# Layer 0's attention: tiles copied by GpSimd DMAs and transposed as fp32r in later turns

## The chip, the cores and the metric

The kernel runs on one core of a Trainium2 chip. The metric is the device time of one execution, in microseconds (us), as the median of several runs. The core has five engines that run their own queues in order and meet at semaphores: TensorE (PE; its weight loads are a row of their own, PEld), VectorE (DVE), ScalarE (ACT), GpSimd (POOL) and SyncE (SP, which here only issues DMAs). SBUF is the on-chip memory of 128 partitions; PSUM is where TensorE writes, in banks of 512 fp32 columns.

## The reference

Two decoder layers on 256 tokens of width 1024, in fp32. Layer 0 uses dilated attention, layer 1 a block-sparse attention (MoBA); a gated feed-forward network with a short convolution follows each. What the change touches is layer 0's attention, cut here to the core:

```python
def mixer_dilated(h, w_qkv, q_gain, k_gain, w_o, cos, sin):
    qkv = (h @ w_qkv).reshape(B, S, 3, N_DIL, N_HEADS, HEAD_DIM)   # 3 groups, 16 heads of 64
    q = apply_partial_rope(rmsnorm(qkv[:, :, 0], q_gain[:, None, :]), cos, sin)
    k = apply_partial_rope(rmsnorm(qkv[:, :, 1], k_gain[:, None, :]), cos, sin)
    v = qkv[:, :, 2]
    ...
    for g, (window, dil) in enumerate(((128, 1), (512, 4), (2048, 16))):
        o, m, d = band_attention(qb[:, g], kb[:, g], vb[:, g], dil, window)
    ...
    wgt = d * jnp.exp(m - m.max(axis=0, keepdims=True))     # the groups, merged by
    wgt = wgt / wgt.sum(axis=0, keepdims=True)              # their softmax denominators
    attn = jnp.einsum('gsh,gshd->shd', wgt, o)

def band_attention(q, k, v, dil, window):   # causal: query t sees keys t, t-dil, ..., t-window
    scores = einsum(q, k) * ATTN_SCALE, masked
    p = exp(scores - max); den = p.sum(-1); o = einsum(p, v) / den
```

Merging the three groups by their denominators is one softmax over the keys of all three, which is how the kernel computes it: 384 columns per query (256 for group 0, 64 and 64 for groups 1 and 2) with one maximum and one sum.

## The kernel before

**Precision.** A product of fp32 matrices is made of three fp32r products: each weight is split into a rounded high part (`whi`, by ACT, L109) and the rest (`wlo`, by DVE, L117), the activations likewise (`xT`). So each block of a product has three matmuls: L456, L457 and L458 (high by high, low by high, high by low).

**Turns.** The program's order is written out by hand as a series of turns. Each calls `turn(fn)`: it starts weight copies, runs what earlier turns put into the table `first` for it, finishes weight splits, runs the table `pre`, then `fn` (12 matmuls with 512 columns), then the table `post`. `at(table, dt, f, ...)` puts a call into a table dt turns ahead. Engines' queues follow this order. In `post`, a key sorts scores and probability products first, then softmax transposes, then transposes of queries and keys.

**Layer 0's attention** goes through 4 sections of 4 heads. A section has a product of queries and keys (128 tokens by 512 columns: 4 heads of queries, 4 of keys) for each of 3 groups and each of 2 chunks of tokens, 2 turns each, and products of values; in all 16 or 20 turns. What follows a product of queries and keys:

- `done`: ACT takes the squares (L539) and copies it from its PSUM bank into a `qk` tile (L533); a turn later `head_sums` (DVE, L544 to L556: sums of squares, rotation), POOL raises the sums to the power −1/2 (L318), and a turn after that `factors` scales the tile (DVE, L565).
- one turn later, in `post`, `transpose` (two in section 0): four 128x128 transposes on TensorE (L580) into one bank, f32, by a matmul with the identity; ACT copies the results out (L610) and DVE makes low parts of group 0's (L618, L616, in `second_parts`, a turn later).

The **softmax** of a section's chunk starts with `step_A` at a fixed turn (scores of group 0 at L682, of groups 1 and 2 at L691, into 4 banks), then `step_E` (DVE masks and takes the maximum, L708, ACT the exponential, L717), `step_R` (DVE divides by the sum, L724), `step_T` (12 transposes of 128x128, L732, four turns after the scores, two in section 3), `step_V` (ACT copies the transposed weights out, L739) and `step_C` (times the values, L764, at a fixed turn). Exponentials of a chunk stand in two `sm` tiles of 384 KB.

**PSUM**: tiles named `acc` rotate over three banks, those named `S` over four, `O` has one. A product of queries and keys and a set of four transposes each take the next `acc` bank (in section 0 some take `S`). A new tile has to wait until the last reader of the tile three before it is done.

The rest of the code around the change, with the profile's line numbers:

Of the kernel before, what the change touches and what calls it, by code (L numbers as in the profile page):

```python
# [10 lines left out]
F32 = mybir.dt.float32  # L11
F32R = mybir.dt.float32r
# [5 lines left out]
P = 128  # L18
D = 1024
# [39 lines left out]
def r32(ap):  # L59
    return ap.bitcast(F32)  # L60
# [81 lines left out]
def trunk_kernel(ctx, tc, x, a_w_qkv, a_w_o, b_w_qkv, b_w_o, ffn_norm, ffn_w_up, ffn_w_down, pack, mask_a, mask_b,  # L142
# [72 lines left out]
    def at(table, dt, fn, *args):  # L215
        table.setdefault(now[0] + dt, []).append((fn, args))
# [35 lines left out]
        nc.scalar.activation(sp.tile([P, 1], F32, name="wt", bufs=1), ones, func)  # L252

    def gain_row(l):
        g = cp.tile([P, D], F32, name="gain", bufs=1)
        nc.gpsimd.dma_start(g, ffn_norm[l:l + 1, :].to_broadcast([P, D]))
        return g

# [20 lines left out]
    load_T(RAW + 1, 1)  # L279


    pk = cp.tile([P, PK], F32, name="pk")
    nc.sync.dma_start(pk[:, 0:264], pack[:, 0:264])
    mA = cp.tile([P, 768], F32, name="mA")
    mB = cp.tile([P, 384], F32, name="mB")
# [3 lines left out]
    cwT = [pk[:, 264 + l * 176:440 + l * 176] for l in range(2)]  # L289
# [160 lines left out]
    def new_acc():  # L450
        return ps.tile([P, 512], F32, name="acc", bufs=3)
# [9 lines left out]
    def attention(xT, norms, ng, g0, mask):  # L461
# [63 lines left out]
        def qk_block(sec, g, res, rq):  # L525
# [33 lines left out]
            def factors(c, qk, rs):  # L559

                h0 = 0 if dil else HS
                if not dil:
                    rq[c] = rs
                t3 = qk.rearrange("p (h d) -> p h d", d=HD)[:, h0:]
                nc.vector.tensor_mul(t3, t3, rs[:, h0:, None].to_broadcast([P, 8 - h0, HD]))  # L565
                at(post, 2 if dil and sec == 0 else 1, transpose, c, qk)

            def transpose(c, qk):
                if c == 0:
                    if dil and g > 0:  # L570
                        res[g] = [bp.tile([P, 2, 2, P], F32R, name="t0", bufs=TB) for _ in range(2)]
                    elif dil:
                        res[g] = [bp.tile([P, 2, 2, S], F32R, name="kT", bufs=QB) for _ in range(2)]
                    else:
                        res[g] = (bp.tile([P, 2, 2, P], F32R, name="t0", bufs=TB),
                                  bp.tile([P, 2, 2, P], F32R, name="t0", bufs=TB),
                                  bp.tile([P, 2, 2, S], F32R, name="kT", bufs=QB))
                tp = ps.tile([P, 512], F32, name="S", bufs=4) if dil and sec == 0 and g < 2 else new_acc()
                for i in range(4):
                    nc.tensor.transpose(tp[:, i * P:(i + 1) * P], qk[:, i * P:(i + 1) * P], ident)  # L580
                q = tp[:, 0:2 * P].rearrange("p (r t) -> p r t", r=2)
                k = tp[:, 2 * P:4 * P].rearrange("p (r t) -> p r t", r=2)
                gk = gqk[:, g0 + g:g0 + g + 1]
                cs = slice(c * P, (c + 1) * P)

                copies, subs = [], []

                def plain(t0):
                    copies.extend(((r32(t0[:, 0]), q, 1.0), (r32(t0[:, 1]), k, gk)))

                def split(hi, lo, src, scale):
                    copies.append((hi, src, 1.0 if scale is None else scale))
                    subs.append((hi, lo, src, scale))


                if dil and g > 0:
                    plain(res[g][c])
                elif dil:
                    qT, kT = res[g]
                    split(kT[:, :, 0, cs], kT[:, :, 1, cs], k, gk)  # L600
                    split(qT[:, 0, :, cs], qT[:, 1, :, cs], q, None)
                else:
                    t0, q1, kT = res[g]
                    split(kT[:, :, 0, cs], kT[:, :, 1, cs], k, gk)
                    if c == 0:
                        plain(t0)
                    else:
                        split(q1[:, 0], q1[:, 1], q, None)
                for o, src, scale in copies:
                    nc.scalar.activation(o, src, AF.Copy, scale=scale)  # L610
                at(first, 1, second_parts, subs)
# [46 lines left out]

            yield from product(done)

        O, weights, starts = {}, {}, []

        def step_A(sec, c, heads, qkT, v, rq):

# [33 lines left out]
            at(first, 2, step_R, heads, sm, den, n)  # L698
            at(post, (2 if sec == NSEC - 1 else 4) if wide else 3 if not dil and sec == NSEC - 1 else 2, step_T, sec, c, heads, v, sm, n)

        def step_E(c, heads, rq, place, n, part, sm, den, mx, nb_):

            t = bp.tile([P, 768], F32, name="sm", bufs=2)
            these = range(len(heads))[part]
            sm.extend(t[:, i * n:(i + 1) * n] for i in range(len(these)))
            for i in these:
                s2, o = place[i]
                nc.vector.tensor_tensor_reduce(  # L708
                    out=sm[i], in0=s2[:, o:o + n], in1=mask[:, c * moff:c * moff + n],
                    op0=ALU.add, op1=ALU.max, scale=1.0, scalar=-3.0e38, accum_out=mx[:, i:i + 1])  # L710
# [6 lines left out]
                nc.scalar.activation(sm[i], sm[i], AF.Exp, bias=nb_[:, i:i + 1],  # L717
                                     scale=1.0 if dil else rq[c][:, heads[i]:heads[i] + 1], accum_out=den[:, i:i + 1])

        def step_R(heads, sm, den, n):  # L720
            rd = sp.tile([P, 4], F32, name="rd", bufs=2)
            nc.vector.reciprocal(rd[:, 0:len(heads)], den[:, 0:len(heads)])
            for i in range(len(heads)):
                nc.vector.tensor_scalar(sm[i], sm[i], rd[:, i:i + 1], None, op0=ALU.mult)  # L724

        def step_T(sec, c, heads, v, sm, n):
            tot = n * len(heads)
            Tp = [ps.tile([P, 512], F32, name="S", bufs=4) for _ in range((tot + 511) // 512)]
            for b in range(tot // P):
                o = b % 4 * P  # L730
                i = b * P % n
                nc.tensor.transpose(Tp[b // 4][:, o:o + P], sm[b * P // n][:, i:i + P], ident)  # L732
            at(pre, 1, step_V, sec, c, heads, v, Tp, tot)

        def step_V(sec, c, heads, v, Tp, tot):
# [286 lines left out]
    at(post, 12, nc.sync.dma_start, pk[:, 264:PK], pack[:, 264:PK])  # L1022
    at(post, 20, nc.sync.dma_start, mB, mask_b)
    aT = attention(xT, norms, NG, 0, mA)
    for c in range(2):
        nc.gpsimd.dma_start(xr[:, c, :], x[0, c * P:(c + 1) * P, :])
    xT = new_T()
# [108 lines left out]
```

## Time and profile before

| | |
|---|---|
| median of 3 runs | 762.57 us (762.27 to 762.66) |
| span of the profiled execution (its own time is not listed beside it) | 760.9 us |
| PE busy | 756.4 us, 99% |
| PEld busy | 635.4 us, 84% |
| DVE busy | 582.3 us, 77% |
| ACT busy | 506.0 us, 67% |
| POOL busy | 69.8 us, 9% |
| transposes of queries and keys (L580) | 128, 272 to 275 ns each |
| transposes of softmax weights (L732) | 144, 275 ns each |

Busy time of PE counts matmuls from start to modelled end; they overlap, so a matmul's duration is longer than the time from its start to the next one's. In a row of a timeline stand the start, the busy time, engine, line, operation, what is written and read (`out<-moving,stationary` for a matmul), the shape, the count, and in brackets how long the engine had been idle before and what released it. The rows of the groups end with busy time, mean duration in ns, and idle time ahead of them.

### The profile page before, as it was taken

How to read it: one execution, taken by the hardware profiler on the slowest of the kernel's cores; microseconds unless marked ns; L12 is line 12 of the kernel's file. 1: busy time of each engine (PE TensorE's matmuls, PEld its weight loads, DVE VectorE, ACT ScalarE, POOL GpSimd, SP SyncE). 2: the span in 40 equal slices, each digit the busy share in tenths (PEclk: the TensorE clock that was granted, in tenths of full speed). 3: DMA queues.
4: the chain of work that ended last, by engine and by line, in shares of the span. 5: the costliest groups of instructions: out<-in, count | busy, mean ns of one | idle time of the engine just before them, and what ended most of it. 6: DMA issues, size and time to landing. Idle time of an engine off the chain costs nothing.

```text
span 760.9 us, 12046 instructions
## 1 busy us (share of the span) xinstructions
PE 756.4 (99%) x4394; PEld 635.4 (84%) x4394; DVE 582.3 (77%) x1123; ACT 506.0 (67%) x887; POOL 69.8 (9%) x77
## 2 busy tenths in 40 slices
PE   9999999999999999999999999999999999999998
PEld 8888888888888888888888888787778888888886
DVE  6887875975786566997887787978866798877874
ACT  7778666757776457676666656777765677566660
POOL 0330120320131000000000001112000000000000
PEclk9999999999999999999999999999999999999999
DMA  9947462562746436487666553743646368666621
GB/s 293 332 141 251 132 186 80 181 217 65 231 158 223 132 90 194 146 251 215 192 193 183 195 190 116 231 139 112 190 116 185 119 186 247 200 178 200 191 100 56
DMA packets 149452, 133.83 MB, mean 176 GB/s; under 512 B 5904, under 2 KB 134544, under 8 KB 149392
## 3 DMA queue, kind: packets, MB, share of 16 engines
q1 hardware_dynamic: 148816, 130.96, 56.0%
q0 software_dynamic: 576, 2.10, 0.7%
q8 instruction: 34, 0.56, 0.3%
q14 instruction: 26, 0.21, 0.1%
HBM read 131.99 MB, written 1.05 MB: 175 GB/s over the span
## 4 chain that ended last, share of the span: by engine, by line
PE 99%; DVE 0%; issue 0%
PE acc L887 14%; PE acc L456 13%; PE acc L458 13%; PE acc L457 13%; PE acc L890 8%; PE S L940 5%; PE S L941 5%; PE S L942 5%; PE O L887 5%; PE O L890 3%; PE O L764 2%; PE acc L513 2%; PE S L732 2%; PE acc L580 2%; PE S L682 2%; PE O L513 1%
## 5 line engine op out<-in xcount | busy, mean ns | idle before, releaser
L117 DVE TENSOR_TENSOR wlo<-raw,whi 128x1024 fp32r<-128x1024 f32 x236 | 283.5, 1217 | 7.0 <-ACT whi L109 6.6
L109 ACT ACTIVATE whi<-raw 128x1024 fp32r<-128x1024 f32 x236 | 244.3, 1054 | 5.7 <-DMA raw<-in_a_w_qkv_dram 2.3
L456 PE MATMUL acc<-whi,xT 128*128 128x512 f32 x424 | 171.8, 405 | 0.0
L458 PE MATMUL acc<-wlo,xT 128*128 128x512 f32 x424 | 165.8, 391 | 0.0
L457 PE MATMUL acc<-whi,xT 128*128 128x512 f32 x424 | 165.4, 390 | 0.0
L887 PE MATMUL acc<-xT,whi 128*128 128x512 f32 x480 | 119.3, 390 | 0.0
L887 PEld LDWEIGHTS acc<-xT,whi 128*128 128x128 f32 x480 | 88.3, 188 | 17.2
L458 PEld LDWEIGHTS acc<-wlo,xT 128*128 128x128 f32 x424 | 79.6, 188 | 17.5
L456 PEld LDWEIGHTS acc<-whi,xT 128*128 128x128 f32 x424 | 79.7, 188 | 16.8 <-issue 1.2
L457 PEld LDWEIGHTS acc<-whi,xT 128*128 128x128 f32 x424 | 79.9, 188 | 14.7
L318 POOL TENSOR_TENSOR rs_y<-rs_v,mhalf 128x8 f32<-128x8 f32 x32 | 53.7, 1681 | 210.9 <-DVE rs_v L316 208.0
L890 PEld LDWEIGHTS acc<-xT,wlo 128*128 128x128 f32 x480 | 65.5, 190 | 4.7
L940 PE MATMUL S<-whi,kT 128*128 128x512 f32 x174 | 68.2, 392 | 0.0
L941 PE MATMUL S<-whi,kT 128*128 128x512 f32 x174 | 68.1, 391 | 0.0
L942 PE MATMUL S<-wlo,kT 128*128 128x512 f32 x174 | 67.7, 389 | 0.0
L890 PE MATMUL acc<-xT,wlo 128*128 128x256 f32 x480 | 66.9, 282 | 0.0
L911 DVE SCALAR_TENSOR_TENSOR qk<-sm,pk,qk 128x255 f32<-128x255 f32 (+1 forms) x160 | 66.6, 476 | 0.4 <-ACT qk L908 0.3
L900 DVE TENSOR_TENSOR sm<-acc,pT 128x256 f32<-128x256 f32 x60 | 25.4, 423 | 46.9 <-ACT pT L899 46.9
L908 ACT ACTIVATE qk<-sm,pk 128x256 f32<-128x256 f32 x80 | 47.8, 598 | 4.0 <-DVE sm L900 3.7
L924 ACT ACTIVATE kT<-qk 128x512 fp32r<-128x512 f32 x22 | 13.9, 633 | 41.2 <-DVE qk L919 41.2
L887 PE MATMUL O<-xT,whi 128*128 128x512 f32 x160 | 40.2, 393 | 0.0
L942 PEld LDWEIGHTS S<-wlo,kT 128*128 128x128 f32 x174 | 32.7, 188 | 7.0
(167 smaller groups left out, 927.5 us busy)
## 6 DMA issues: line engine op xcount, KB each, us to landing
raw<-in_ffn_w_up_dram SPq DMA_DIRECT2D x80, 512.0 KB, 4.2
raw<-in_a_w_qkv_dram SPq DMA_DIRECT2D x144, 256.0 KB, 4.3
raw<-in_ffn_w_down_dram SPq DMA_DIRECT2D x44, 512.0 KB, 3.8
raw<-in_b_w_qkv_dram SPq DMA_DIRECT2D x48, 256.0 KB, 3.5
raw<-in_a_w_o_dram SPq DMA_DIRECT2D x8, 512.0 KB, 3.8
raw<-in_ffn_w_up_dram SPq DMA_DIRECT2D x16, 256.0 KB, 3.6
raw<-in_b_w_o_dram SPq DMA_DIRECT2D x8, 512.0 KB, 3.8
xr<-in_x_dram POOLq DMA_DIRECT2D x2, 512.0 KB, 5.9
```

The source lines that it names most:

```text
L109: self.nc.scalar.activation(hi, raw, AF.Copy)
L117: self.nc.vector.tensor_sub(lo, self.raw[self.done], r32(hi))
L318: nc.gpsimd.tensor_tensor(y, v, mhalf[:, 0:n], op=ALU.pow)
L456: nc.tensor.matmul(acc, T[:, k, 0, cs], hi, start=first, stop=False)
L457: nc.tensor.matmul(acc, T[:, k, 1, cs], hi, start=False, stop=False)
L458: nc.tensor.matmul(acc, T[:, k, 0, cs], lo, start=False, stop=last)
L887: nc.tensor.matmul(acc, hi[:, k], xT[:, k].rearrange("p j t -> p (j t)"), start=(k == 0), stop=False)
L890: nc.tensor.matmul(acc[:, S:2 * S], lo[:, k], xT[:, k, 0], start=False, stop=(k == 7))
L911: nc.vector.scalar_tensor_tensor(o[:, d:S], u[:, 0:S - d], cw[:, first_tap + b:first_tap + b + 1], o[:, d:S], op0=ALU.mult, op1=ALU.add)
L940: nc.tensor.matmul(o, acts[f][:, 0, cs], hi[:, sl], start=start, stop=False)
L941: nc.tensor.matmul(o, acts[f][:, 1, cs], hi[:, sl], start=False, stop=False)
L942: nc.tensor.matmul(o, acts[f][:, 0, cs], lo[:, sl], start=False, stop=stop)
```

## The change

In sections 1 to 3 the scaled tile of queries and keys is no longer transposed where it stands. `move` copies it by a DMA that POOL issues (256 KB, SBUF to SBUF) into another `qk` tile of type fp32r, and the transposes read that, two turns later (three for group 0), with an identity of type fp32r. So they stand four turns (five for group 0) behind `done`'s product rather than three. Group 2 of section 3 and all of section 0 stay as they were. In sections 0 to 2 `step_M` copies the two divided softmax tiles in the same way (384 KB each, into new tiles `pL`), and `step_T` comes 5 turns (first chunk) or 6 (second) after the scores rather than 4. Section 3's softmax and layer 1 stay.

Beside this, tiles are put together to make room: the identity is drafted in a `qk` buffer and cast to fp32r by DVE, the gain row takes a `kT` buffer, the small tables a `pT` buffer, both masks one buffer, and layer 1's tables of rotations are made at turn 12, not 40.

```diff
-    ident = cp.tile([P, P], F32, name="ident")
-    make_identity(nc, ident)
+    draft = bp.tile([P, 512], F32, name="qk", bufs=5)[:, 0:P]
+    make_identity(nc, draft)
+    ident_r = cp.tile([P, P], F32R, name="ident")
+    nc.vector.tensor_copy(ident_r, draft)
+    ident = r32(ident_r)
...
-                at(post, 2 if dil and sec == 0 else 1, transpose, c, qk)
-
-            def transpose(c, qk):
+                if not dil or sec == 0 or g == 2 and sec == NSEC - 1:
+                    at(post, 2 if dil and sec == 0 else 1, transpose, c, qk, ident)
+                else:
+                    at(post, 0, move, c, qk)
+
+            def move(c, qk):
+                moved = bp.tile([P, 512], F32R, name="qk", bufs=5)
+                nc.gpsimd.dma_start(r32(moved), qk)
+                at(post, 2 if g else 3, transpose, c, moved, ident_r)
+
+            def transpose(c, qk, one):
...
+                to = tp if one is ident else tp.bitcast(F32R)
                 for i in range(4):
-                    nc.tensor.transpose(tp[:, i * P:(i + 1) * P], qk[:, i * P:(i + 1) * P], ident)
+                    nc.tensor.transpose(to[:, i * P:(i + 1) * P], qk[:, i * P:(i + 1) * P], one)
...
-            at(post, (2 if sec == NSEC - 1 else 4) if wide else 3 if not dil and sec == NSEC - 1 else 2, step_T, sec, c, heads, v, sm, n)
+            moved = [] if dil and sec < NSEC - 1 else None
+            at(first, 2, step_R, heads, sm, den, n, moved)
+            at(post, (2 if sec == NSEC - 1 else 5 + c) if wide else 3 if not dil and sec == NSEC - 1 else 2, step_T, sec, c, heads, v, sm, n, moved)
...
+        def step_M(sm, n, moved):
+            for i in range(0, len(sm), 2):
+                t = bp.tile([P, 768], F32R, name="pL", bufs=2)
+                moved.extend(t[:, j * n:(j + 1) * n] for j in range(2))
+                nc.gpsimd.dma_start(r32(t), box_of[id(sm[i + 1])])
...
-                nc.tensor.transpose(Tp[b // 4][:, o:o + P], sm[b * P // n][:, i:i + P], ident)
+                to = Tp[b // 4][:, o:o + P]
+                nc.tensor.transpose(to if moved is None else to.bitcast(F32R), src[b * P // n][:, i:i + P], one)
...
-    at(post, 40, gain_tables, 1, nc.gpsimd)
+    at(post, 12, gain_tables, 1, nc.gpsimd)
```

Where instructions move, the order of each engine's queue tells. First TensorE in section 1, at the end of the product of group 2's first chunk (`acc_1179` before, `acc_1191` after) and the start of its second chunk's (`acc_1262`, `acc_1264`); numbers tell tiles of one name apart. Before:

```order
L456 MATMUL acc_1179<-whi_1051,xT_126 128x512
L457 MATMUL acc_1179<-whi_1051,xT_126 128x512
L458 MATMUL acc_1179<-wlo_1052,xT_126 128x512
L456 MATMUL acc_1262<-whi_948,xT_126 128x512
L457 MATMUL acc_1262<-whi_948,xT_126 128x512
L458 MATMUL acc_1262<-wlo_949,xT_126 128x512
```

After:

```order
L459 MATMUL acc_1191<-whi_1055,xT_128 128x512
L460 MATMUL acc_1191<-whi_1055,xT_128 128x512
L461 MATMUL acc_1191<-wlo_1056,xT_128 128x512
L592 MATMUL acc_1239<-ident_90,qk_1166 128x128 x4
L459 MATMUL acc_1264<-whi_959,xT_128 128x512
L460 MATMUL acc_1264<-whi_959,xT_128 128x512
```

Four transposes of group 1 now stand between the two products; the `acc` tiles taken around here are 1111, 1124 (transposes), 1179, 1209 (transposes), 1262 before, and 1191, 1204 (transposes), 1239 (transposes), 1264 after. So the tile three before the second chunk's is a set of transposes before, and the first chunk's product after.

Next VectorE in section 2, at the scaling of group 1's second chunk (`qk_1817` before, `qk_1841` after). Before:

```order
L565 TENSOR_TENSOR qk_1750<-qk_1750,rs_y_1767 128x512
L618 SCALAR_TENSOR_TENSOR kT_1702<-acc_1789,gqk_125,kT_1702 128x2x128
L616 TENSOR_TENSOR kT_1701<-acc_1789,kT_1701 128x2x128
...
L117 TENSOR_TENSOR wlo_1797<-raw_1538,whi_1796 128x1024
L117 TENSOR_TENSOR wlo_1800<-raw_1570,whi_1799 128x1024
L565 TENSOR_TENSOR qk_1817<-qk_1817,rs_y_1831 128x512
L117 TENSOR_TENSOR wlo_1822<-raw_1646,whi_1821 128x1024
```

After:

```order
L117 TENSOR_TENSOR wlo_1821<-raw_1569,whi_1820 128x1024
L117 TENSOR_TENSOR wlo_1824<-raw_1601,whi_1823 128x1024
L568 TENSOR_TENSOR qk_1841<-qk_1841,rs_y_1857 128x512
L630 SCALAR_TENSOR_TENSOR kT_1808<-acc_1883,gqk_127,kT_1808 128x2x128
L628 TENSOR_TENSOR kT_1807<-acc_1883,kT_1807 128x2x128
L117 TENSOR_TENSOR wlo_1848<-raw_1673,whi_1847 128x1024
```

The low parts of group 0's second chunk (`acc_1789`, `acc_1883`) have moved from behind one scaling to behind the next, and in section 2 their bank is the one that group 2's second product takes over.

Last ScalarE at the end of section 1, where group 2's transposes are copied out (`t_1342`, `t_1391`: second chunk; `v`: values copied out, `xT<-O`: the attention's output of section 0). Before:

```order
L633 ACTIVATE v_1370<-acc,rn_r_392 128x256
L636 ACTIVATE v_797<-acc,rn_r_392 64x256 x2
L610 ACTIVATE t_1342<-acc 128x256
L610 ACTIVATE t_1342<-acc,gqk 128x256
L109 ACTIVATE whi<-raw 128x1024 x2
L444 ACTIVATE xT<-O 128x2x2x64 x2
L717 ACTIVATE sm,den<-sm,nbias 128x384 x4
```

After:

```order
L109 ACTIVATE whi<-raw 128x1024 x2
L447 ACTIVATE xT<-O 128x2x2x64 x2
L731 ACTIVATE sm,den<-sm,nbias 128x384 x4
L645 ACTIVATE v_1520<-acc,rn_r_394 128x256
L648 ACTIVATE v_859<-acc,rn_r_394 64x256 x2
L622 ACTIVATE t_1391<-acc 128x256
L622 ACTIVATE t_1391<-acc,gqk 128x256
```

The second chunk's copies have moved from ahead of two weight copies, the output and the exponentials to behind them.

More of the change, by code (lines that the diff above doesn't have):

```diff
@@ L254, in gain_row @@
     def gain_row(l):
-        g = cp.tile([P, D], F32, name="gain", bufs=1)
+        g = bp.tile([P, D], F32, name="kT", bufs=QB)
         nc.gpsimd.dma_start(g, ffn_norm[l:l + 1, :].to_broadcast([P, D]))
@@ L279, in trunk_kernel @@
     load_T(RAW + 1, 1)
-    pk = cp.tile([P, PK], F32, name="pk")
+    pk = bp.tile([P, 768], F32, name="pT", bufs=4)
     nc.sync.dma_start(pk[:, 0:264], pack[:, 0:264])
-    mA = cp.tile([P, 768], F32, name="mA")
-    mB = cp.tile([P, 384], F32, name="mB")
+    taps = cp.tile([P, PK - 264], F32, name="taps")
+    mA = bp.tile([P, 768], F32, name="mask", bufs=1)
     gcol = pk[:, 0:8].rearrange("p (j g) -> p j g", j=2)
@@ L288, in trunk_kernel @@
     gbf = pk[:, 136:264].rearrange("p (m d) -> p m d", d=16)
-    cwT = [pk[:, 264 + l * 176:440 + l * 176] for l in range(2)]
+    cwT = [taps[:, l * 176:176 + l * 176] for l in range(2)]
     CG = cp.tile([P, 2, 4, 2, 16], F32, name="CG")
@@ L659, in v_last @@
             yield from product(done)
-        O, weights, starts = {}, {}, []
+        O, weights, starts, box_of = {}, {}, [], {}
         def step_A(sec, c, heads, qkT, v, rq):
@@ L697, in step_A @@
                 at(pre if i and sec < NSEC - 1 else first, 1, step_E, c, heads, rq, place, n, slice(i, i + 2 if wide else len(heads)), sm, den, mx, nb_)
-            at(first, 2, step_R, heads, sm, den, n)
-            at(post, (2 if sec == NSEC - 1 else 4) if wide else 3 if not dil and sec == NSEC - 1 else 2, step_T, sec, c, heads, v, sm, n)
+            moved = [] if dil and sec < NSEC - 1 else None
+            at(first, 2, step_R, heads, sm, den, n, moved)
+            at(post, (2 if sec == NSEC - 1 else 5 + c) if wide else 3 if not dil and sec == NSEC - 1 else 2, step_T, sec, c, heads, v, sm, n, moved)
         def step_E(c, heads, rq, place, n, part, sm, den, mx, nb_):
@@ L705, in step_E @@
             sm.extend(t[:, i * n:(i + 1) * n] for i in range(len(these)))
+            box_of[id(sm[-1])] = t
             for i in these:
@@ L718, in step_E, with step_R @@
                                      scale=1.0 if dil else rq[c][:, heads[i]:heads[i] + 1], accum_out=den[:, i:i + 1])
-        def step_R(heads, sm, den, n):
+        def step_R(heads, sm, den, n, moved):
             rd = sp.tile([P, 4], F32, name="rd", bufs=2)
@@ L724, in step_R, with step_T @@
                 nc.vector.tensor_scalar(sm[i], sm[i], rd[:, i:i + 1], None, op0=ALU.mult)
-        def step_T(sec, c, heads, v, sm, n):
+            if moved is not None:
+                at(post, 0, step_M, sm, n, moved)
+        def step_M(sm, n, moved):
[3 more added lines that the diff above has]
+                nc.gpsimd.dma_start(r32(t), box_of[id(sm[i + 1])])
+        def step_T(sec, c, heads, v, sm, n, moved):
+            src, one = (sm, ident) if moved is None else (moved, ident_r)
             tot = n * len(heads)
@@ L1018, in trunk_kernel @@
     at(post, 6, norm.sums)
-    at(post, 40, gain_tables, 1, nc.gpsimd)
+    at(post, 12, gain_tables, 1, nc.gpsimd)
     at(post, 7, norm.factors)
     at(post, 8, nc.sync.dma_start, mA, mask_a)
-    at(post, 12, nc.sync.dma_start, pk[:, 264:PK], pack[:, 264:PK])
-    at(post, 20, nc.sync.dma_start, mB, mask_b)
+    at(post, 12, nc.sync.dma_start, taps, pack[:, 264:PK])
     aT = attention(xT, norms, NG, 0, mA)
+    mB = bp.tile([P, 768], F32, name="mask", bufs=1)
+    at(post, 20, nc.sync.dma_start, mB[:, 0:384], mask_b)
     for c in range(2):
```

## The prediction

> **What bounds the kernel now.** I read the busy line and the chain of waits first, then the groups by form on TensorE (PE), then the timelines around the places that the change touches.
>
> ```profile
> span 760.9 us, 12046 instructions
> PE 756.4 (99%) x4394; PEld 635.4 (84%) x4394; DVE 582.3 (77%) x1123; ACT 506.0 (67%) x887; POOL 69.8 (9%) x77
> PE 99%; DVE 0%; issue 0%
> 135.00:140.00 5.00, 5.00 (x62) 4.03 (x61) 4.97 (x11) 3.15 (x6) 3.65 (x5) 1.00 0.73 233
> ```
>
> PE is busy for 756.4 of 760.9 us and the chain is 99% PE: whatever shortens PE's own work shortens the kernel, one for one, and any microsecond in which PE has to wait is lost one for one. The last line (a five-microsecond window in layer 0: length, then PE, PEld, DVE, ACT, POOL busy, granted clock, DMA share, GB/s) shows that DVE, at 77% on average, is full here (4.97 of 5.00). So in layer 0 a wait for DVE is near even where none shows. The clock is 1.00 there, so durations are at full speed.
>
> **The gain: cheaper transposes.** The moved sections have 16 blocks of queries and keys with 4 transposes each, and 6 softmax steps with 12 each: 136 transposes become fp32r. A transpose multiplies the tile (stationary) by a moving identity of 128 columns, so its price is that of 128 moving columns, unless loading the stationary operand takes longer.
>
> ```profile
> L764 PE MATMUL O<-pT,v 128*64 128x128 f32 x224 | 17.2, 277 | 0.0
> L764 PE MATMUL O<-pT,v 128*64 128x64 f32 x128 | 6.4, 221 | 0.0
> L887 PE MATMUL acc<-xT,whi 128*128 128x512 f32 x480 | 119.3, 390 | 0.0
> L890 PE MATMUL acc<-xT,wlo 128*128 128x256 f32 x480 | 66.9, 282 | 0.0
> 67.62 0.39 PE L458 MATMUL acc<-wlo,xT 128*128 128x512 f32 x1
> 67.85 1.47 PE L732 MATMUL S<-ident,sm 128*128 128x128 f32 x12
> 69.39 0.40 PE L457 MATMUL acc<-whi,xT 128*128 128x512 f32 x1
> 97.88 0.39 PE L458 MATMUL acc<-wlo,xT 128*128 128x512 f32 x1
> 98.11 0.39 PE L456 MATMUL acc<-whi,xT 128*128 128x512 f32 x1
> 287.28 1.12 PE L890 MATMUL acc<-xT,wlo 128*128 128x256 f32 x8
> 288.24 0.60 PE L867 MATMUL S<-ident,qk 128*128 128x128 f32 x4
> ```
>
> A duration is not the price, since matmuls overlap; the price is the pitch from start to start. Two fp32r products with 512 columns stand 0.23 us apart (97.88 to 98.11). From 67.62 to 69.39, 12 f32 transposes lie among two such products (one at 67.62, one just ahead of 69.39): 1.77 − 2 × 0.23 = 1.31 us, 109 ns each. Eight fp32r products with 256 columns take 288.24 − 287.28 = 0.96 us, 120 ns each. A column costs (277 − 221)/64 = 0.875 ns in f32 and (390 − 282)/256 = 0.42 ns in fp32r. So an fp32r transpose with 128 columns should have a pitch of 120 − 128 × 0.42 = 66 ns, going down from the row with 256 columns, or 109 − 128 × (0.875 − 0.42) = 51 ns, going down from the f32 transposes. I take 66, since its row is of the new type: 136 × 43 = **−5.9 us**; with 51 it is −7.9.
>
> ```profile
> L732 PEld LDWEIGHTS S<-ident,sm x144: 138/140/143, 67.6 to 558.2; 128*128 128x128 f32 x144
> L890 PEld LDWEIGHTS acc<-xT,wlo x480: 187/192/192, 287.1 to 740.6; 128*128 128x128 f32 x160
> 112.77 2.90 PE L764 MATMUL O<-pT,v 128*64 128x128 f32 x64
> ```
>
> What can undo this is the load. The f32 transposes' loads take 140 ns each and the fp32r ones 192 ns (minimum, median, maximum in each row), and yet those with 192 run at a pitch of 120. So loads overlap, and the pitch that they allow lies at or below 120, not in view. The nearest rows below are the 64 small products of L764: 2.90/64 = 45 ns each with a 64-column load, so 90 ns for 128 columns at most. The gain then has a floor: pitch 120 would cost 136 × 11 = +1.5 us, pitch 90 would bring −2.6. [...]
>
> **The new waits on PSUM banks.** Moving a transpose also changes which earlier tile its neighbours inherit a bank from. There are three "acc" banks, in rotation. In sections 1 and 3 the last product of group 2 (second chunk) took over the bank of an early transpose; now two transposes stand between, and it takes over the bank of the product that ended just ahead of it. PE must wait until ACT has copied that product out (squares, then copy).
>
> ```profile
> 98.64 0.64 ACT L539 ACTIVATE sq<-acc 128x512 f32<-128x512 f32 x1
> 99.11 0.65 ACT L533 ACTIVATE qk<-acc 128x512 f32<-128x512 f32 x1
> 219.66 0.39 PE L458 MATMUL acc<-wlo,xT 128*128 128x512 f32 x1
> 220.89 0.65 ACT L533 ACTIVATE qk<-acc 128x512 f32<-128x512 f32 x1
> ```
>
> The product's last matmul ends at 97.88 + 0.39 = 98.27, the copy at 99.76: 1.49 us, and in section 3 the same (220.05, 221.54). The four transposes that PE has in between fill 4 × 66 ns = 0.26, and the first matmul needs some 0.1 to start: 1.35 us lost, in two sections **+2.7 us**. Bounds: 1.2 each, or 2.4 each if ACT is one weight copy late (L109, below). Queued behind the waiting matmul is all of PE.
>
> In section 2 the same product waits for DVE instead: for the two subtractions L618, L616 on the moved transposes of group 0, which now stand behind one more scaling (L565).
>
> ```profile
> 135.50 0.97 PE L682 MATMUL S<-kT 64*128 64x256 f32 x12
> 139.65 0.55 DVE L708 CUSTOM_DVE_ANT_0 sm<-S,mA 128x384 f32<-128x384 f32 x1
> 145.27 0.18 DVE L722 RECIPROCAL rd<-den 128x4 f32<-128x4 f32 x1 [1.38 <-ACT sm L717]
> 149.65 0.69 DVE L565 TENSOR_TENSOR qk<-qk,rs_y 128x512 f32<-128x512 f32 x1
> 154.78 0.68 DVE L565 TENSOR_TENSOR qk<-qk,rs_y 128x512 f32<-128x512 f32 x1
> 153.70 0.39 PE L456 MATMUL acc<-whi,xT 128*128 128x512 f32 x1
> 117.88 0.38 ACT L610 ACTIVATE t<-acc 128x256 f32<-128x256 f32 x1 [6.40 <-PE acc L580]
> ```
>
> Count from the scores at 135.50, section 1's second chunk. PE came to the product in question at 153.70, 18.2 us later; of the 24 f32 transposes in between, 12 move out and 12 get cheaper: 18.2 − 24 × 0.109 + 12 × 0.066 = 16.4. DVE has the same instructions as before from the first mask (139.65) to the end of the scaling (154.78 + 0.68 = 155.46): 15.8 us. It began 4.15 us after the scores, because it was behind; ACT's stall of 6.40 us ahead of it (117.88, ACT in its queue ahead of the weight copies that DVE needs) goes, since those transposes now stand behind the scores and their copies behind the exponentials. So I let DVE begin 1.3 us after the first score matmul (0.97 us of scores and a start): 1.3 + 15.8 + 0.25 (PE's restart) = 17.4, against 16.4: **+1.0 us**. Bounds: 0 (the 1.38 us that DVE waited at 145.27 shrink) and 3.8 (DVE begins as late as before).
>
> **The copies.** Each moved tile goes through a DMA of 256 KB (16 of them, queries and keys) or 384 KB (12, softmax), issued by POOL, which is 91% idle. What one takes is not in the trace; the nearest rows:
>
> ```profile
> xr<-in_x_dram POOLq DMA_DIRECT2D x2, 512.0 KB, 5.9
> gain<-in_ffn_norm_dram POOLq DMA_DIRECT2D x2, 512.0 KB, 7.2
> L109 ACT ACTIVATE whi<-raw 128x1024 fp32r<-128x1024 f32 x236 | 244.3, 1054 | 5.7 <-DMA raw<-in_a_w_qkv_dram 2.3
> out_dram<-xr SPq DMA_DIRECT2D x3, 256.0 KB, 2.0
> 80.18 0.97 PE L682 MATMUL S<-kT 64*128 64x256 f32 x12
> 92.61 0.69 DVE L565 TENSOR_TENSOR qk<-qk,rs_y 128x512 f32<-128x512 f32 x1
> 127.02 1.41 DVE L724 TENSOR_SCALAR sm<-sm,rd 128x384 f32<-128x384 f32 x4
> 128.61 1.47 PE L732 MATMUL S<-ident,sm 128*128 128x128 f32 x12
> ```
>
> 256 KB landed in 2.0 us from SP's queue, 512 KB in 5.9 to 7.2 from POOL's; I take 4.0, midway to the lower. The tightest place is section 1: the scaling ends at 92.61 + 0.69 = 93.30, less 0.81 for a pair L618, L616 that now stands behind it: 92.5. PE ends the product ahead at 98.27 − 24 × 0.109 + 8 × 0.066 = 96.2 (counted from the scores at 80.18, as above) and then waits for its bank until 97.5 anyway. So a landing of up to 97.5 − 0.26 − 92.5 = 4.7 us costs nothing more, and each microsecond beyond costs one, in sections 1 and 3. In section 2 the same transposes have 1 us more. The softmax copies start at 127.02 + 1.41 = 128.4; PE took the tiles at 128.61 and now takes them a turn (12 products, 2.73 us) or two later: 131.3 for the first chunk, where 4.0 us lets them land at 132.4, but the 6.40 us that ACT no longer stalls lie in this very chain. Nothing, at most 1.1 in each of sections 1 and 3; the second chunk has 2.7 more. ACT's copies of later products into the five "qk" buffers, and DVE's next masks into "sm", wait for landings of three products and ten turns ago: nothing.
>
> **What else moves.**
>
> ```profile
> 3.52 0.48 DVE L397 SCALAR_TENSOR_TENSOR xT<-xr,xT 128x256 fp32r<-128x256 f32 x1 [2.52 <-ACT xT L396]
> L318 POOL TENSOR_TENSOR rs_y<-rs_v,mhalf 128x8 f32<-128x8 f32 x32 | 53.7, 1681 | 210.9 <-DVE rs_v L316 208.0 <-DVE rb L554 2.9
> q1 hardware_dynamic: 148816, 130.96, 56.0%
> ```
>
> The draft of the identity and its cast stand at the start, where DVE waits 2.52 us for data; the gain row, the small tables and masks in shared buffers load when these are idle; gain_tables(1) fills POOL at turn 12 rather than 40, where POOL waits for DVE (208.0 us ahead of L318 alone): nothing in each case. The 28 copies add 16 × 256 + 12 × 384 KB = 8.7 MB to the 131 MB of the weights' queue, whose packets fill 56% of the DMA engines' time.
>
> **Sum** against the profiled execution, of which the page gives the span alone: −5.9 + 2.7 + 1.0 = −2.2 us, 760.9 → 758.7. The median of the runs, 762.57, lies 1.7 above that span; I take these 1.7 us to stay: **760.4 us**. Its own range is 758.5 to 763 (pitch 51 and no wait in section 2; both waits at their ends and a late softmax copy). A change within 0.2%, 1.5 us, cannot be told from none.
>
> **Rivals.**
>
> *Loads set the pitch* (slower). If a transposed fp32r load cannot be started every 66 ns, the waits stay and the gain doesn't. For it: 192 against 140 ns in the load rows; and 128 f32 columns cost 128 × 0.875 = 112 ns, so that at 109 a limit just below could not be seen. Against it: 45 ns for a 64-column load. At an unchanged 109 the sum is 0 + 3.7: 766.3; at 120 it is 767.8. It decides from a pitch of 109 − 3700/136 = 82 ns on: beyond that the kernel is slower than before.
>
> *Copies land late* (slower). Landing at 7.2, the gain row: 2.5 us more in sections 1 and 3, 1.5 in section 2: 766.9; at 5.9 it is 763.0. I take 764.9; it decides from 5.8 us on. [...] Against: half the bytes. [...]
>
> *The waits don't come* (faster still). DVE and ACT run ahead, so that the bank is free 1.2 us after each product and section 2 doesn't wait, at a pitch of 51: −7.9 + 2.4 = −5.5, 757.1.
>
> **Chances.** Forecast .48, loads .20, late copies .15, no waits .12, anything else .05 (half of it slower). Faster by over 0.2% (below 761.0): .33 of the forecast, .12, .01: .46. Within: .13 of the forecast, .04 of the copies, .03 of the loads, .02: .22. Slower (above 764.1): .17 of the loads, .11 of the copies, .02 of the forecast, .02: .32. From 757.4 to 767.4 the range takes in the rivals but for their ends, and leaves out about 2 in 10.
>
> **What the profile after would show.** [...] PE idle ahead of the first matmul of group 2's second chunk, 1.3 us for ACT's copy in sections 1 and 3, about 1 for DVE in section 2; if it is the transposes that wait for a DMA, copies were late. ACT without its 6.40 us stall. The DMA rows of "qk" and "pL" near 4 us to landing. I would be wrong above all if the pitch is over 82 ns or the landing over 5.8 us.

## The result and the profile after

The changed kernel takes 767.91 us as the median of 6 runs, against 762.5 before; the ratio is 1.006 (95% interval 1.0049 to 1.0071). In a second job it took 768.25 (766.99 to 769.54) beside 762.69, ratio 1.0074 (1.0061 to 1.0087). The forecast was 760.4, with 767.4 as the upper end of the range. The first profile fell on an execution whose granted clock was 0.85 from end to end (span 826.3), so the lines below are from the changed kernel in the second job. Its line numbers are those of the changed code: L592 and L756 are the transposes (L580 and L732 before), L459 to L461 the products (L456 to L458).

The head of the page and the chain of waits:

```profile
span 766.5 us, 12167 instructions
PE 755.8 (99%) x4394; PEld 632.7 (83%) x4394; DVE 583.3 (76%) x1124; ACT 508.0 (66%) x887; POOL 83.5 (11%) x105
PE 88%; DMA 5%; DVE 3%; issue 2%; ACT 2%; POOL 0%; SPq 0%; DVEq 0%; POOLq 0%; ACTq 0%
```

The span is 5.6 us longer while PE's busy time is no longer than before (756.4 then). The chain was 99% PE; now 12% of it runs through others. Busy shares alone would not show this: the chain does. PE's waits (us in all, times, longest):

```profile
PE acc L592 <- DMA qk<-qk: 3.5, 2, 2.4
PE acc L592 <- DVE kT L628: 2.1, 1, 2.1
```

Before, layer 0's sections had none. PE's timeline has them at the three places that the prediction named, at the end of the product of group 2's first chunk in sections 1, 2 and 3, but ahead of the transposes of group 1's first chunk that stand there:

```profile
96.31 0.39 PE L461 MATMUL acc<-wlo,xT 128*128 128x512 f32 x1
98.81 0.51 PE L592 MATMUL acc<-ident,qk 128*128 128x128 f32 x4 [2.12 <-DVE kT L628]
...
99.92 0.55 PE L459 MATMUL acc<-whi,xT 128*128 128x512 f32 x1
100.27 0.63 PE L460 MATMUL acc<-whi,xT 128*128 128x512 f32 x1
...
103.57 0.64 PE L756 MATMUL S<-ident,pL 128*128 128x128 f32 x6
...
154.71 0.39 PE L461 MATMUL acc<-wlo,xT 128*128 128x512 f32 x1
156.14 0.51 PE L592 MATMUL acc<-ident,qk 128*128 128x128 f32 x4 [1.04 <-DMA qk<-qk]
...
221.32 0.39 PE L461 MATMUL acc<-wlo,xT 128*128 128x512 f32 x1
224.13 0.51 PE L592 MATMUL acc<-ident,qk 128*128 128x128 f32 x4 [2.42 <-DMA qk<-qk]
```

In section 1 the profile names DVE's subtraction L628, but it was the copy there too. These are L628 in sections 1 and 2:

```profile
98.35 0.42 DVE L628 TENSOR_TENSOR kT<-acc,kT 128x256 fp32r<-128x256 f32 x1
155.79 0.41 DVE L628 TENSOR_TENSOR kT<-acc,kT 128x256 fp32r<-128x256 f32 x1
```

In section 1 it ended at 98.77, and the copy, issued at 93.57, landed after 5.1 us, at 98.7: the two nearly coincide. In section 2 the transposes started at 156.14, before L628 had ended (156.20), so they do not need it there; and in section 1 PE starts 0.04 us behind its end, where elsewhere it takes 0.14 to start behind such a subtraction (152.77 to 152.91 and 98.72 to 98.86 in kernels below). In the f32 version below, the profile names the copy in all three places.

From start to start, less the usual 0.23 us, PE loses 2.27, 1.20 and 2.58 us: 6.05. Then something that was in no part of the prediction's sum: from 99.92 to 103.57 nine products take 3.65 us, 0.41 each rather than 0.23. The stretches' row says why (length, busy times, then the granted clock):

```profile
100.10:103.40 3.30, 3.30 (x9) 2.52 (x9) 3.12 (x8) 1.07 (x2) 1.66 (x1) 0.50 0.95 304
103.60:107.00 3.40, 3.40 (x24) 2.97 (x23) 0.00 (x0) 2.48 (x5) 0.57 (x1) 1.00 0.77 252
```

From 1.2 us after the first wait on, PE's clock stood at 0.50 for about 3.4 us, and 3.65 − 9 × 0.23 = 1.6 us were lost. The gain is there too, at less than half its size. Twelve fp32r softmax transposes between two products, and four of queries and keys:

```profile
70.90 0.39 PE L461 MATMUL acc<-wlo,xT 128*128 128x512 f32 x1
71.13 1.14 PE L756 MATMUL S<-ident,pL 128*128 128x128 f32 x12
72.11 0.47 PE L459 MATMUL acc<-whi,xT 128*128 128x512 f32 x1
72.41 0.40 PE L460 MATMUL acc<-whi,xT 128*128 128x512 f32 x1
...
230.88 0.39 PE L461 MATMUL acc<-wlo,xT 128*128 128x512 f32 x1
231.11 0.46 PE L592 MATMUL acc<-ident,qk 128*128 128x128 f32 x4
231.41 0.46 PE L459 MATMUL acc<-whi,xT 128*128 128x512 f32 x1
231.71 0.39 PE L460 MATMUL acc<-whi,xT 128*128 128x512 f32 x1
```

72.41 − 70.90 − 2 × 0.23 = 1.05 us, 88 ns each; 231.71 − 230.88 − 2 × 0.23 = 0.37, 93 ns each, where f32 had 109 and 111. That is 72 × 21 + 64 × 18 ns = 2.7 us. The account of this execution: −2.7 + 6.05 + 1.6 = +4.95; another 0.6 was lost in the first 26 us of the program, ahead of the sections; measured +5.6.

### The profile page after: what moved, and what is told of

Same layout as the page of the kernel before. It is cut to its first block, busy times and chain, and to the rows that moved or that the text cites. A ratio compares the mean times of both kernels' runs of the same rounds, so it can differ in the third digit from the quotient of the medians.

```text
span 826.3 us, 12167 instructions
## 1 busy us (share of the span) xinstructions
PE 820.5 (99%) x4394; PEld 653.3 (79%) x4394; DVE 584.9 (71%) x1124; ACT 511.6 (62%) x887; POOL 83.6 (10%) x105
## 3 DMA queue, kind: packets, MB, share of 16 engines
HBM read 131.99 MB, written 1.05 MB: 161 GB/s over the span
## 4 chain that ended last, share of the span: by engine, by line
PE 99%; ACT 0%; DVE 0%; issue 0%
PE acc L911 15%; PE acc L459 14%; PE acc L461 13%; PE acc L460 13%; PE acc L914 7%; PE S L965 5%; PE S L964 5%; PE S L966 5%; PE O L911 5%; PE O L914 2%; PE O L788 2%; PE acc L516 2%; PE S L756 2%; PE S L694 1%; PE acc L592 1%; PE S L460 1%
## 5 line engine op out<-in xcount | busy, mean ns | idle before, releaser
L459 PE MATMUL acc<-whi,xT 128*128 128x512 f32 x424 | 182.7, 431 | 0.2
L461 PE MATMUL acc<-wlo,xT 128*128 128x512 f32 x424 | 176.7, 417 | 0.0
L460 PE MATMUL acc<-whi,xT 128*128 128x512 f32 x424 | 176.4, 416 | 0.0
L911 PE MATMUL acc<-xT,whi 128*128 128x512 f32 x480 | 130.4, 417 | 0.0
L461 PEld LDWEIGHTS acc<-wlo,xT 128*128 128x128 f32 x424 | 81.4, 192 | 24.0
L459 PEld LDWEIGHTS acc<-whi,xT 128*128 128x128 f32 x424 | 81.4, 192 | 23.7 <-issue 1.4
L460 PEld LDWEIGHTS acc<-whi,xT 128*128 128x128 f32 x424 | 81.8, 193 | 20.7
L965 PE MATMUL S<-whi,kT 128*128 128x512 f32 x174 | 72.8, 419 | 0.0
L964 PE MATMUL S<-whi,kT 128*128 128x512 f32 x174 | 72.5, 417 | 0.0
L966 PE MATMUL S<-wlo,kT 128*128 128x512 f32 x174 | 72.2, 415 | 0.0
L935 DVE SCALAR_TENSOR_TENSOR qk<-sm,taps,qk 128x255 f32<-128x255 f32 (+1 forms) x160 | 66.6, 477 | 0.4
L932 ACT ACTIVATE qk<-sm,taps 128x256 f32<-128x256 f32 x80 | 47.8, 597 | 2.9 <-DVE sm L924 2.7
L923 ACT ACTIVATE pT<-acc 128x256 f32<-128x256 f32 x60 | 22.8, 380 | 34.8 <-PE acc L914 33.1
L547 DVE TENSOR_REDUCE qssq<-sq 128x8 f32<-128x512 f32 x32 | 21.8, 682 | 31.8 <-ACT sq L542 31.8
```

Source lines behind the costliest of these rows:

```text
L459: nc.tensor.matmul(acc, T[:, k, 0, cs], hi, start=first, stop=False)
L460: nc.tensor.matmul(acc, T[:, k, 1, cs], hi, start=False, stop=False)
L461: nc.tensor.matmul(acc, T[:, k, 0, cs], lo, start=False, stop=last)
L911: nc.tensor.matmul(acc, hi[:, k], xT[:, k].rearrange("p j t -> p (j t)"), start=(k == 0), stop=False)
L935: nc.vector.scalar_tensor_tensor(o[:, d:S], u[:, 0:S - d], cw[:, first_tap + b:first_tap + b + 1], o[:, d:S], op0=ALU.mult, op1=ALU.add)
L964: nc.tensor.matmul(o, acts[f][:, 0, cs], hi[:, sl], start=start, stop=False)
```

## The experiments

Each is the changed kernel with the edit shown, unless another base is named.

**The changed kernel again.**

> The changed kernel itself, once more, for a profile at full clock (the first one was taken at a granted clock of 0.85, span 826.3). Theory W (new waits eat the gain): fp32r transposes stand 60 to 75 ns apart, and PE waits some 8 us in layer 0, for copies and for banks. Rival L (loads set the pitch): the transposes stand 100 ns or more apart and the waits come to 3 to 4 us. Rival K (clock): the waits come to under 4 us and the transposes are cheap, but the granted clock falls below 1.00 in stretches and costs the rest. Time 765.4 to 769 in all.

768.25. None of the three theories had it whole: the pitch lies between W's and L's, the waits between W's 8 us and L's 4, and K's fall of the clock comes on top. The five runs' granted clocks were 0.995 to 0.998, and the times followed them: 766.99 at 0.998, 769.54 at 0.996. Two runs of the first job at 1.000 took 765.45 and 765.92. That is about 762.5 − 2.7 + 6.05 = 765.9, the account without a half-clock stretch. So the scatter of this kernel, 4 us where the kernel before has under 1, follows the granted clock (0.995 to 1.000): as I read it, half-clock stretches that come or stay away. The profile of one execution, at 0.997, has one.

**Copies kept, fp32r left out.**

```diff
-                moved = bp.tile([P, 512], F32R, name="qk", bufs=5)
-                nc.gpsimd.dma_start(r32(moved), qk)
-                at(post, 2 if g else 3, transpose, c, moved, ident_r)
+                moved = bp.tile([P, 512], F32, name="qk", bufs=5)
+                nc.gpsimd.dma_start(moved, qk)
+                at(post, 2 if g else 3, transpose, c, moved, ident)
...
-                t = bp.tile([P, 768], F32R, name="pL", bufs=2)
+                t = bp.tile([P, 768], F32, name="pL", bufs=2)
...
-            src, one = (sm, ident) if moved is None else (moved, ident_r)
+            src, one = (sm, ident) if moved is None else (moved, ident)
...
-                nc.tensor.transpose(to if moved is None else to.bitcast(F32R), src[b * P // n][:, i:i + P], one)
+                nc.tensor.transpose(to, src[b * P // n][:, i:i + P], one)
```

> All copies and all moved turns stay, but the copied tiles are f32 and are transposed as f32. W: the waits stay and the gain of 136 x 43 ns goes, some 772 (a little less, since later PE waits less). L: no different from the changed kernel, 767. K: if the clock falls because of the fp32r transposes, full clock and 764 to 768.

768.85 (768.48 to 771.48), clock 0.995 to 1.000. The half-clock stretches are here too (0.51 from 99.9 to 103.4 us; 0.92 over 100 to 120 us and 0.91 over 220 to 240), so fp32r doesn't cause them. PE waits for the copy in all three places:

```profile
PE acc L592 <- DMA qk<-qk: 4.9, 3, 2.1
```

The medians are only 0.6 us apart, but they lie at different granted clocks (0.997 for the changed kernel, 0.999 here). At a granted clock of 1.000 two runs of this kernel took 768.48 and 768.55, and two of the changed one 765.45 and 765.92, in another job: so fp32r is worth some 2.8 us in this order too, as far as two runs each can tell.

**fp32r kept, copies and turns left out.** DVE's own scaling and division write the fp32r tiles (`to` is a new `qk` tile, `o` part of a `pL` tile), and `transpose` and `step_T` run in the turns of before.

```diff
-                nc.vector.tensor_mul(t3, t3, rs[:, h0:, None].to_broadcast([P, 8 - h0, HD]))
+                nc.vector.tensor_mul(to, t3, rs[:, h0:, None].to_broadcast([P, 8 - h0, HD]))
...
-                    at(post, 0, move, c, qk)
+                    at(post, 1, transpose, c, moved, ident_r)
...
-                nc.vector.tensor_scalar(sm[i], sm[i], rd[:, i:i + 1], None, op0=ALU.mult)
+                nc.vector.tensor_scalar(o, sm[i], rd[:, i:i + 1], None, op0=ALU.mult)
```

> No copies and the turns of before: DVE's scaling (queries and keys) and division (softmax) write an fp32r tile themselves, which rounds the values, and the same 136 transposes are fp32r. W: the gain without the waits, 762.5 - 5.9 = 756.6 (755 to 758). L: 762 to 764. K: 757 to 761, with the granted clock below 1.00 in the runs that are late.

760.52 (760.05 to 760.72), ratio 0.997 (0.996 to 0.9981): a gain of 2.2, not 5.9. From the start of 12 of its transposes to the next product it is 0.98 us (67.45 to 68.43), as in the changed kernel (71.13 to 72.11), so the copies have no part in that. Waits of 0.2 us each at two places make up most of the rest to 2.7.

**The same tiles, in the change's turns.** Base: the kernel just above.

```diff
-                    at(post, 1, transpose, c, moved, ident_r)
+                    at(post, 2 if g else 3, transpose, c, moved, ident_r)
...
-            at(post, (2 if sec == NSEC - 1 else 4) if wide else 3 if not dil and sec == NSEC - 1 else 2, step_T, sec, c, heads, v, sm, n, moved)
+            at(post, (2 if sec == NSEC - 1 else 5 + c) if wide else 3 if not dil and sec == NSEC - 1 else 2, step_T, sec, c, heads, v, sm, n, moved)
```

> No copies (DVE writes the fp32r tiles), but all transposes in the turns of the change. Theory B (the turns alone: banks and DVE) has the prediction's waits: about 1.1 to 1.4 us each in sections 1 and 3 for ACT's copy of the product ahead, 0 to 1 in section 2, none for a DMA; 762.7 - 2.75 (the gain that the traces show) + 2.5 to 3.5 = 762.5 to 763.5. Theory D (the copies' landing is all of the waits): no wait, 760.0, like the kernel with the turns of before.

763.05 (ratio 1.0005, 0.9996 to 1.0014). The turns alone give back the whole gain, as theory B had it; PE's waits:

```profile
PE acc L459 <- ACT qk L536: 1.8, 2, 0.9
PE acc L459 <- DVE kT L626: 1.0, 1, 1.0
```

These are the prediction's bank waits, in their three places: 0.9 us each where it had 1.35, and 1.0 where it had 1.0. So 2.8 us are the banks'; what the copies add to that, up to the changed kernel's 6.05, the next experiments show.

**Softmax alone; queries and keys alone.** The first:

```diff
-                if not dil or sec == 0 or g == 2 and sec == NSEC - 1:
+                if True:
```

> Only the softmax tiles are copied (12 copies of 384 KB) and transposed as fp32r a turn or two later; queries and keys as before. W, with the loss in the queries' and keys' part as the prediction had it: 762.5 - 72 x 0.043 = 759.4, no wait. If the loss lies in the softmax part (late copies, S banks held longer): 763 or more. L: 762.5 to 764.

The second:

```diff
-            moved = [] if dil and sec < NSEC - 1 else None
+            moved = None
...
-            at(post, (2 if sec == NSEC - 1 else 5 + c) if wide else 3 if not dil and sec == NSEC - 1 else 2, step_T, sec, c, heads, v, sm, n, moved)
+            at(post, (2 if sec == NSEC - 1 else 4) if wide else 3 if not dil and sec == NSEC - 1 else 2, step_T, sec, c, heads, v, sm, n, moved)
```

> The change for queries and keys alone (16 copies of 256 KB, the change's turns); softmax as before. If the three waits come from that part: they stay, a little longer or shorter since PE's other transposes are back, 4 to 7 us in all, against a gain of 16 x 73 ns = 1.2; with no, one or two stretches at half clock of 1.7 us each, 766 to 770. If the softmax copies ahead of them in GpSimd's queue make the copies late: two thirds of the waits or less, 763 to 766.

763.99 (1.0017, 1.0008 to 1.0026) and 764.13 (1.0017, 1.0008 to 1.0026). Alone they lose 1.3 and 1.5 us, together 5.6. Alone, the softmax part gains 72 × 21 ns = 1.5 us and waits 2.3 us for its own copies. Clocks were 0.999 to 1.000 in every run. Softmax alone, then queries and keys alone:

```profile
PE S L756 <- DMA pL<-sm: 2.3, 2, 1.2
```

```profile
PE acc L459 <- DVE kT L628: 2.3, 3, 1.2
```

With queries and keys alone no transpose waits for a copy; only the banks are left. (Here the count of three banks in rotation doesn't hold: in section 1 the product started at 98.86, while ACT was still reading the product ended before, 98.75 to 99.40, and the profile names DVE's subtraction, which ended at 98.72.) The difference next to group 2's second product is in one copy, that of group 1's first chunk. GpSimd's timeline in section 1, the changed kernel ahead of queries and keys alone:

```profile
92.16 1.11 POOL L746 DMA_DIRECT2D pL<-sm  x2
93.57 0.54 POOL L576 DMA_DIRECT2D qk<-qk  x1 [0.30 <-ACT whi L109]
```

```profile
93.52 0.60 POOL L576 DMA_DIRECT2D qk<-qk  x1 [1.37 <-ACT whi L109]
```

The copy goes out at the same time, but from issue to landing it takes 5.1 us in the first and 2.9 in the second (in sections 2 and 3, 5.0 and 5.4 in the first, 2.9 and 3.9 in the second). What differs is 768 KB of softmax ahead of it, issued from 1.4 us before it on.

**Softmax copies two turns later**, so that they stand behind that copy.

```diff
-                at(post, 0, step_M, sm, n, moved)
+                at(post, 2, step_M, sm, n, moved)
```

> The change with the softmax copies issued two turns later, so that group 1's copy stands ahead of them in GpSimd's queue instead of right behind them. If it is the 768 KB just ahead that make that copy land after 5.0 to 5.4 us (2.9 where queries and keys alone are copied): it lands in 3 us, its transposes no longer wait for it, PE's waits there fall from 6.0 us to the banks' 2.8 or less, and no stretch at half clock is left. The softmax copies themselves may then be up to 1 us late in each of three places. 762.7 - 2.75 + 2.8 to 5 = 762.7 to 765. If it lands after 5 us all the same: as the change, 766 to 769.

776.82 (1.0186): much slower than I expected, and yet the point shows. That copy lands after 2.8 us in all three sections, and the waits next to it are the banks' again (0.9, 1.0 and 0.8). But the softmax copies now stand behind the next power on GpSimd, which waits for DVE, and their transposes wait:

```profile
PE S L756 <- DMA pL<-sm: 8.8, 6, 3.8
PE acc L459 <- ACT qk L536: 1.7, 2, 0.9
PE acc L459 <- DVE kT L628: 1.0, 1, 1.0
```

**Copies issued by SP.**

```diff
-                nc.gpsimd.dma_start(r32(moved), qk)
+                nc.sync.dma_start(r32(moved), qk)
...
-                nc.gpsimd.dma_start(r32(t), box_of[id(sm[i + 1])])
+                nc.sync.dma_start(r32(t), box_of[id(sm[i + 1])])
```

> The change with its 28 copies issued by SP rather than by GpSimd (turns as in the change). Theory D: what is late is GpSimd's queue (each copy of queries and keys stands behind two softmax copies and a power) and its 5 us to land; from SP 256 KB may land in 2 to 4.5 us, and of the waits those of the banks stay, 1.1 to 1.4 each: 762 to 764. Against it: SP's copy waits for DVE at the head of SP's queue and holds back the weights behind it, and landing stays at 4.5 us: 766 and more.

775.58 (1.0167). From SP the copies land in much the same time (median; GpSimd's had 4.3 and 5.0):

```profile
pL<-sm SPq DMA_DIRECT2D x12, 384.0 KB, 4.8
qk<-qk SPq DMA_DIRECT2D x16, 256.0 KB, 4.6
```

The copy of group 1's first chunk took 4.2, 4.1 and 5.0 us, against 5.1, 5.0 and 5.4, and PE waited as long for it (2.0, 0.9 and 2.3). So GpSimd as the issuer is at most a small part of what makes landing slow. From SP the copies go out behind weight loads (95.76 rather than 93.57 in section 1), and softmax transposes wait for them six times (4.8 us in all).

**What sets the 88 ns.** Base: the kernel in which DVE writes the tiles.

```diff
-                nc.tensor.transpose(to if moved is None else to.bitcast(F32R), src[b * P // n][:, i:i + P], one)
+                blk = src[b * P // n][:, i:i + P]
+                if moved is not None and sec == 0:
+                    nc.tensor.matmul(to, blk, one, start=True, stop=True)
+                elif moved is not None and sec == 1 or dil and sec == NSEC - 1 and c == 0:
+                    for h in (0, 64):
+                        nc.tensor.matmul(to[:, h:h + 64], blk, one[:, h:h + 64], start=True, stop=True)
+                else:
+                    nc.tensor.transpose(to if moved is None else to.bitcast(F32R), blk, one)
```

> What sets the 88 ns between fp32r transposes: DVE writes the tiles, turns of before. Softmax transposes of section 0 are plain matmuls with the identity; those of section 1, and the f32 ones of section 3's first chunk, are pairs of plain matmuls with 64 moving columns each, each with the whole tile as its stationary operand (loaded twice). If the load sets the pitch: 85 to 90 ns from one half to the next in fp32r (a set of 12 takes twice as long), and 90 or more in f32. If the moving columns set it: 45 to 60 ns in both. Section 0's plain matmuls: as the transposes, 81 to 89.

One run, 768.64 us. PE's timeline, section 0 (12 whole blocks as plain fp32r matmuls), section 1 (fp32r halves, 24 of them), section 2 (12 fp32r transposes) and section 3 (f32 halves, 48), each with the next product, and the load rows (ns, minimum, median, maximum) of halves and of transposes:

```profile
67.50 1.45 PE L753 MATMUL S<-ident,pL 128*128 128x128 f32 x12
68.78 0.45 PE L459 MATMUL acc<-whi,xT 128*128 128x512 f32 x1
...
127.85 2.76 PE L756 MATMUL S<-ident,pL 128*128 128x64 f32 x24
130.44 0.49 PE L459 MATMUL acc<-whi,xT 128*128 128x512 f32 x1
...
187.04 1.14 PE L758 MATMUL S<-ident,pL 128*128 128x128 f32 x12
188.01 0.47 PE L459 MATMUL acc<-whi,xT 128*128 128x512 f32 x1
...
244.31 5.46 PE L756 MATMUL S<-ident,sm 128*128 128x64 f32 x48
249.58 0.48 PE L459 MATMUL acc<-whi,xT 128*128 128x512 f32 x1
```

```profile
L756 PEld LDWEIGHTS S<-ident,pL x48: 188/192/192, 127.6 to 151.9; 128*128 128x128 f32 x48
L758 PEld LDWEIGHTS S<-ident,pL x24: 138/140/142, 186.8 to 218.7; 128*128 128x128 f32 x24
```

From the start of a set to the next product it is 1.28/12 = 107 ns for a whole plain block, 2.59/24 = 108 for an fp32r half and 5.27/48 = 110 for an f32 half. Half the moving columns, the same pitch: the moving columns don't set it, and what each half has in full is its load (192 ns in its row). So I take the load of the stationary tile to set the pitch of these plain matmuls, in both types. No run changes the load alone; the small products of L764, with a stationary tile of 64 columns, stood at 45 ns. Both numbers that I had expected (85 to 90 for halves, 81 to 89 for section 0) were too low. A transpose in fp32r stands closer than these: 0.97/12 = 81 ns counted in this way, 88 counted as above. Its load row has 140 ns rather than 192, but so has that of the f32 transposes, which stand at 109. What holds fp32r transposes at 88 this experiment doesn't show.

**Group 1's transposes one turn later.**

```diff
-                at(post, 2 if g else 3, transpose, c, moved, ident_r)
+                at(post, 3 if g < 2 else 2, transpose, c, moved, ident_r)
```

> The change with one number altered: group 1's copied tiles are transposed three turns after the copy, not two, behind the first turn of group 2's second product instead of ahead of it. That takes the late copy off PE's path and also gives that product a bank that no product has just left. Both theories: the three waits of 1.2 to 2.6 us go and with them the stretches at half clock; 762.7 - 2.75 = 760.0 (759.5 to 761). If the copies still land too late elsewhere: 761 to 764. If the clock falls without those waits: above 761.5 at a granted clock of 0.998 or less.

759.61 us (759.24 to 759.92), ratio 0.996 (0.9946 to 0.9974): faster than both kernels. Group 1's transposes now stand behind the first turn of group 2's second product, so the copy has 2.7 us more, and by the order the bank that this product takes is that of an earlier set of transposes. PE has no wait in layer 0's sections, and the chain is PE's again:

```profile
span 757.5 us, 12166 instructions
PE 99%; DMA 1%; SPq 0%; ACT 0%; DVE 0%; issue 0%
98.17 0.39 PE L461 MATMUL acc<-wlo,xT 128*128 128x512 f32 x1
98.40 1.14 PE L756 MATMUL S<-ident,pL 128*128 128x128 f32 x12
99.37 0.50 PE L592 MATMUL acc<-ident,qk 128*128 128x128 f32 x4
```

**The same order in f32**, with the edit of the second experiment.

> The version with group 1's transposes a turn later, with f32 copies and f32 transposes: what fp32r itself is worth where nothing waits. If it is 136 transposes at 88 to 93 ns against 110: 759.6 + 2.75 = 762.4 (762.0 to 762.8). If the prediction's 66 ns were right somewhere: 765.5.

762.75 (1.0003, 0.9994 to 1.0012). Where nothing waits, fp32r alone is worth 762.75 − 759.61 = 3.1 us, 23 ns for each of 136 transposes.

## Why the prediction was wrong

- **The gain** was the first term that failed: 136 × 43 = 5.9 us by a pitch of 66 ns; measured 88 to 93 ns inside the kernel, 2.7 us from the rows and 3.1 on the chip. I took the price from the moving columns, because the row with 256 columns was of the new type. The halves show that this price doesn't hold for such small matmuls: plain ones stand at 107 to 110 ns with 64 moving columns and with 128. My bound from the 45 ns of the small products, "90 ns for 128 columns at most", is refuted for them; that fp32r transposes came to 88 is luck for it, since what holds those is open. The rival that loads set the pitch came nearest, with −2.6 us for a pitch of 90, and its mechanism fits the plain matmuls alone. I had looked for a limit above 82 ns to make the kernel slower, and held that less likely than no limit.
- **The bank waits** stood where the prediction put them: 0.9, 1.0 and 0.9 us where nothing else is late, against 1.35, 1.0 and 1.35. ACT was sooner there: before, it copied softmax weights (L739) until 98.64 us, 0.4 us past that product's end at 98.27, and now it stands idle for 1.09 us ahead of that product's squares (at 96.21 us in the kernel in which DVE writes the tiles in the change's turns). PE's start behind the reader, which I had put at 0.1 us behind ACT and 0.25 behind DVE without a row, took 0.05 (L536 ended at 97.30, the product started at 97.35) and 0.14 there (L626 ended at 152.77, the product started at 152.91).
- **The copies** were the second term that failed. I took 4.0 us to land, worked out that up to 4.7 was free, and named the place. It took 5.0 to 5.4 there, and the copy went out 0.6 us after the scaling had ended. With group 1's transposes one turn later, nothing else changed, these waits are gone and the kernel takes 759.61. The step at fault priced each copy alone, from rows of single transfers, though GpSimd issues two softmax copies of 384 KB right ahead of it: 2.9 us became 5.1. So 6.05 us of waits rather than 3.7.
- **The clock** was missing, a term put at nothing without a reason: I wrote that any wait is lost one for one. The wait in section 1 cost 2.27 us and 1.6 more at half clock.
- Put together, −2.7 + 6.05 + 1.6 (+0.6 at the start) instead of −5.9 + 3.7. The terms that failed all did so on the same side, so two rivals came true at once, each in part, and their sum lies outside a range made for one at a time. The sums had slips as well: the forecast's own terms, pitch 51 and no wait in section 2 at one end, all waits at their ends and late softmax copies at the other, add up to 757.4 and 767.5, not to 758.5 and 763.
- **Right** were the identity, the shared buffers and tables (nothing, as the version with no waits shows) and ACT's stall of 6.40 us, which is gone (the longest wait for such transposes is now 1.8).

## What to carry to other kernels

When work is moved to a later turn on a full engine, follow it through three things, not one: the data it needs, the PSUM bank that it and its neighbours take over, and what is queued on the issuing engine right ahead of its transfer; here one turn more for one group was worth over 8 us. Price a small matmul by its stationary load as well as by its moving columns (here plain ones stood at 107 to 110 ns with 64 moving columns and with 128), and look for a row whose moving operand is shorter than its load. Terms that lean on each other (softmax copies ahead of a copy that then lands after 5.1 us rather than 2.9, a wait of 2.27 us with a stretch at half clock behind it) don't add up: the two halves of this change cost 1.3 and 1.5 us alone, and 5.6 together.

## What the hardware did that I had not expected

- After a wait of 2.27 us PE ran at a granted clock of 0.50 for about 3.4 us. The wait of 2.58 us in section 3 of the same execution had no such stretch behind it (1.00 over 220 to 240 us); in the f32 copy version the waits in sections 1 and 3 both had one (0.92 over 100 to 120 us and 0.91 over 220 to 240). So the length of the wait alone doesn't decide, and what does no run here shows.
- A stretch at half clock also came with no wait at all, in the kernel with 24 halves of 108 ns and four transposes between two products:

```profile
149.44 2.76 PE L756 MATMUL S<-ident,pL 128*128 128x64 f32 x24
152.03 0.54 PE L590 MATMUL acc<-ident,qk 128*128 128x128 f32 x4
152.40 0.74 PE L459 MATMUL acc<-whi,xT 128*128 128x512 f32 x1
152.50:156.00 3.50, 3.50 (x10) 2.76 (x10) 3.28 (x4) 3.21 (x7) 0.47 (x1) 0.52 0.52 160
```

  Here three microseconds of short matmuls without a wait were followed by a granted clock of 0.52, about what came behind the wait. It isn't a rule: in the same execution the 24 halves from 127.85 on and the 48 from 244.31 on were followed by a clock of 1.00 (products 0.22 to 0.24 us apart right behind them), and its mean clock of 0.998 has room for this one stretch alone.
- The copy of 256 KB from SBUF to SBUF in these three places landed after 2.8 us with the softmax copies behind it and 2.9 to 3.9 with none in the kernel, and after 5.0 to 5.4 with 768 KB issued from 1.4 us before it on. That isn't all that slows copies: with no softmax copy in the kernel, the 16 copies took 2.8 to 5.9 us, median 4.3. From SP's queue the median was 4.6 us, from GpSimd's 5.0.
